# Scheduling priority for the RWKV chains, solves and chunk operands of a hybrid mLSTM and RWKV-7 layer

## Chip, cores and metric

The kernel runs on one core of a Trainium2 chip. The metric is the device time of one execution in microseconds (us), here the median of the runs. Engines: PE = TensorE (matmuls), DVE = VectorE, ACT = ScalarE, POOL = GpSimd, SP = SyncE, whose queue issues the DMAs.

## What is computed

One layer of a diffusion backbone with 512 latent tokens (x), 256 context tokens (ctx) and a width of 2048. Cut to what matters:

```python
sh1, sc1, gt1, sh2, sc2, gt2 = adaln(c, w_mod, b_mod)         # six vectors of 2048; w_mod is 2048 x 12288
hc = modulate(rms_norm(ctx, g_norm1), csh1, csc1)
_, ctx_state = hybrid_mixers(hc, p, zero_state)
hx = modulate(rms_norm(x, g_norm1), sh1, sc1)
yx, _ = hybrid_mixers(hx, p, ctx_state)
x = x + gt1 * (yx @ w_out)
x = x + gt2 * conv_ffn(modulate(rms_norm(x, g_norm2), sh2, sc2))
return rms_norm(x, g_final)

def hybrid_mixers(h, p, state):
    proj = h @ p["w_in"]                  # all inputs of both head groups
    ...                                   # 4 mLSTM heads, 16 RWKV-7 heads, both in two directions

def rwkv7_step(s, r, w, k, v, kk, a):     # for each token and head, state 64 x 64
    s = s * w[None, :] - (s @ kk)[:, None] * (kk * a)[None, :] + v[:, None] * k[None, :]
    return s, s @ r
```

## The kernel before

All data are fp32. A dense product splits the weights and the tokens into a high and a low part and takes three matmuls (`proj` L362 ff. with the lines L370 to L372, `proj_tm` with L403 to L405 and others). The weights come through `wload` (L337): a DMA into `wraw`, then the split into `whi` on ACT (L299) and `wlo` on DVE (L300).

RWKV runs over pairs of heads (8 pairs) and chunks of 64 tokens in these stages:

- `pair_shared` and `prep` (L680) make a pair's operands for all chunks: decays from a scan (`r_cum`), exponentials, and the products of chunk operands (`r_Gp`, L747). They store them in DRAM as `Sx_d` (latent tokens) or `Sc_d` (context).
- `tsolve` (L777) inverts the triangular matrices of four units at once: eight loads into `t_X`, thirty steps of two DVE operations each (L798 multiplies, L799 adds), eight stores (L801). Then, for each pair, it loads `t_Y` (L808), transposes on DVE (L810), and joins the halves by small matmuls on PE (L816, L821) with the copy L823, and stores (L824).
- `chain` (L903) runs the recurrence. `chain_v` loads the values, `chain_load` (L826) loads `r_GK` for two chunks, and `chain_step` (L841) computes one chunk in three dependent groups of 64x64 matmuls (L856, L859), with copies to `r_Rs` and `r_U` on ACT (L872, L880) between them. The state `r_M` (L892) and the outputs `r_yt` (L899, L901) are updated on DVE.
- `finalize_pair` (L944) normalises a pair's outputs.

The six vectors of `adaln` come from two kinds of code. The first come early from PE. The others are `ada_late` (L219) chunks: eight loads `am` (L228, one buffer) from `w_mod`, each followed by two DVE products into `adacc` (L230, L232), and at the end a sum over partitions on PE (L238) with L239 on DVE. The sum of a chunk is issued when two later chunks are waiting.

Which job comes when is set by `ctx_job` and `x_job` and the main loop at the end of the mixers. Within a job the program is not the order on the engines: the scheduler of the Tile framework lists all operations by simulated time, and among ready ones takes those with the higher priority, by default the earlier in the program. `tc.high_priority(n)` puts what is inside it n places ahead of its place in the program. In the kernel before, `wload` uses it with 3000 (`AHEAD`, `AHEAD_X`). Each engine then works through its own list in order.

After the last dense projection of the inputs come the last chain, the four mLSTM heads (L540; head 0 runs beside the last chain: L605, L609, L621, L641), the output projection (L1262 ff.) and the convolution FFN.

Of the kernel before, what the change touches and what calls it, by code (L numbers as in the profile page):

```python
# [15 lines left out]
P = 128  # L16
# [70 lines left out]
FIN_O = 1  # L87
EARLY_AT = (1, 2, 4, 4)
PRELOAD = True
TCOPT = dict(schedule_with_timeline_sim=True)  # L90


# [4 lines left out]
def body(tc, A, dbg=None):  # L97
# [5 lines left out]
    def nm(s):  # L103
        cnt[0] += 1
        return f"{s}_{cnt[0]}"
# [25 lines left out]
    def DT(tag, shape, bufs=1):  # L131
        return dr.tile(list(shape), F32, tag=tag, name=nm(tag), bufs=bufs)
# [31 lines left out]
    def V(name, j=0, n=1):  # L164
        o = VO[name] + j
        return vecs[:, o:o + n]
# [74 lines left out]
    def ln_exp():  # L241

        if PRELOAD:
            tc.keep_in_program_order(act.preload_act_table_set("natural_log_exp_and_others"))
# [414 lines left out]
    def pair_shared(p, seg):  # L659
        n = NX if seg == "x" else NC_  # L660
        s = K()
        s.kr = rp("r_kr", [P, NX])
        s.kk = rp("r_kk", [P, NX])
        sp.dma_start(s.kr[:, :n], kr_d[seg][p])
        act.activation(s.kk[:, :n], s.kr[:, :n], AF.Copy, scale=V("rkk", p))
        sq = rp("r_t1", [P, NX])
        act.activation(sq[:, :n], s.kk[:, :n], AF.Square)
        pn = PS("pre", [P, 512])
        pe.matmul(pn[:, :n], bones, sq[:, :n], start=True, stop=True)
        act.activation(sq[:, :n], pn[:, :n], AF.Ln, bias=BK12)  # L670
        act.activation(sq[:, :n], sq[:, :n], AF.Exp, scale=-0.5)
        dve.tensor_tensor(s.kk[:, :n], s.kk[:, :n], sq[:, :n], ALU.mult)
        if seg == "x":
            s.r = rp("r_r", [P, NX])
            sp.dma_start(s.r, r_d[p])
        s.up = rp("r_up", [P, 2, 2, P])
        sp.dma_start(s.up, A["rup"][p])
        return s
# [147 lines left out]
    def chain_load(u, tt):  # L826

        cu = u.c0 + 2 * tt
        o = rk("r_GK", [P, 2, 512], 6)[:, :, 0:3 * u.kc + 128]
        sp.dma_start(o, u.S_d[:, cu:cu + 2, :])  # L830
        return o

    def chain_v(p, seg, nch):

        t = rk("r_V", [P, 8, 64], 3)[:, 0:nch]
        for h, hs in enumerate(LOHI):
            o = (p % 2) * 128 + 64 * h
            sp.dma_start(t[hs], v_d[seg][p // 2, :, :, o:o + 64].rearrange("a (b t) v -> t (a b) v", t=64))
        return t

    def chain_step(us, ops, cs, V, y, first, last):  # L841

        x = us[0].seg == "x"
        kc = us[0].kc
        bank = [PS("R", [P, 8, 64]) for _ in range(2)]
        pos = (0, 1) if cs[0] < cs[1] else (1, 0)
        opened = {}

        def mm(h, half, o, w, rhs):

            hs = LOHI[h]
            out = bank[h][LOHI[half], o, :]
            at = opened.get((h, half))
            f = dict(stop=True, skip_group_check=True)
            if at is None:
                opened[(h, half)] = pe.matmul(out, w[hs], rhs[hs], start=True, **f)  # L856
                return
            with tc.issue_after(at.ins):
                pe.matmul(out, w[hs], rhs[hs], start=False, **f)  # L859

        w = [o[:, c % 2] for o, c in zip(ops, cs)]
        kinds = range(2) if x else range(1)
        for src in range(2):
            for k, u in enumerate(us):
                for j in kinds:
                    for h in range(2):
                        o = 2 * kc * src + 64 * j
                        mm(h, h if j == 0 else 1 - h, pos[k], w[k][:, o:o + 64], u.M if src == 0 else V[:, cs[k], :])
        Rs = rk("r_Rs", [P, 2, 64], 3)
        U = rk("r_U", [P, 2, 64], 3)  # L870
        for h, hs in enumerate(LOHI):
            act.copy(Rs[hs], bank[h][hs, 0:2, :])  # L872
        for k, u in enumerate(us):
            for h in range(2):
                mm(h, 1 - h, 2 + pos[k], w[k][:, kc:kc + 64], Rs[:, pos[k], :])
            for h in range(2):
                if not last:
                    mm(h, h, 2 + pos[k], w[k][:, 3 * kc + 64:3 * kc + 128], V[:, cs[k], :])
        for h, hs in enumerate(LOHI):
            act.copy(U[hs], bank[h][LOHI[1 - h], 2:4, :])  # L880
        for k, u in enumerate(us):
            for h in range(2):
                if not last:
                    mm(h, h, 2 + pos[k], w[k][:, 3 * kc:3 * kc + 64], U[:, pos[k], :])
            for h in range(2):
                if x:
                    mm(h, 1 - h, pos[k], w[k][:, kc + 64:kc + 128], U[:, pos[k], :])
        if not last:
            for k, u in enumerate(us):
                g = u.g0 + cs[k]  # L890
                for h, hs in enumerate(LOHI):
                    dve.scalar_tensor_tensor(u.M[hs], u.M[hs], u.gC[hs, g:g + 1], bank[h][hs, 2 + pos[k], :], ALU.mult, ALU.add)  # L892
        if x:
            lo, hi = min(cs), max(cs)
            for h in range(2):
                hs = LOHI[1 - h]
                out = y[hs, lo:hi + 1:hi - lo, :]
                if first:
                    dve.tensor_copy(out, bank[h][hs, 0:2, :])  # L899
                else:  # L900
                    dve.tensor_tensor(out, bank[h][hs, 0:2, :], out, ALU.add)  # L901

    def chain(pairs, mid):  # L903

        x = pairs[0][0].seg == "x"
        nch = pairs[0][0].nch
        Vs, ys = [], []
        for us in pairs:
            Vs.append(chain_v(us[0].p, us[0].seg, nch))
            ys.append(rk("r_yt", [P, 8, 64], 2) if x else None)  # L910
            for u in us:
                if not x:
                    Mst[(u.p, u.d)] = rk("r_M", [P, 64], 16)
                    pool.memset(Mst[(u.p, u.d)], 0.0)
                u.M = Mst[(u.p, u.d)]
        n = nch // 2
        for i in range(n):
            if x and i == 1:
                mid()
            ops = [[chain_load(u, i if u.d == 0 else n - 1 - i) for u in us] for us in pairs]  # L920
            for c in range(2 * i, 2 * i + 2):
                for us, o, V, y in zip(pairs, ops, Vs, ys):
                    chain_step(us, o, (c, nch - 1 - c), V, y, c < nch // 2, x and c == nch - 1)
        if x:
            for us, y in zip(pairs, ys):
                y_d = us[0].y_d = DT("yr_d", [4, P, 128], 8)
                for h in range(2):
                    sp.dma_start(y_d[:, :, 64 * h:64 * h + 64].rearrange("a (b t) v -> t (a b) v", t=64), y[LOHI[1 - h]])
            mid()

    def bonus(p, uf, ub, s):
        kd = uf.kd
        dve.tensor_tensor(kd, kd, ub.kd, ALU.add)
        dve.tensor_tensor(kd, kd, s.r, ALU.mult)
        rk2 = rk("r_rk2", [P, 2], 2)
        pool.tensor_scalar(rk2, bones2, V("rrk", p), None, ALU.mult)
        pb = PS("pre", [P, 4, 2])
        for tt in range(4):
            pe.matmul(pb[:, tt, :], kd[:, 128 * tt:128 * tt + 128], rk2, start=True, stop=True)
        bo = rk("r_bo", [P, 8], 6)  # L940
        act.copy(bo, pb.rearrange("p a b -> p (a b)"))
        return bo
# [140 lines left out]
    for q, (k0, k1) in enumerate(KPARTS):  # L1083
        ks = slice(k0, k1)
        n = (k1 - k0) * P
# [53 lines left out]
    def do_solve(n=1):  # L1139
        if len(solve_q) >= n:  # L1140
            jobs = [solve_q.pop(0) for _ in range(n)]
            tsolve([us for job in jobs for _, us, _ in job])
            chain_q.extend(jobs)

    def ctx_job(p):
        do_chain()
        job = []
        for pp in range(p, p + 2):
            s = pair_shared(pp, "c")
            job.append((pp, prep(pp, s, "c", DT("Sc_d", [P, 8, 320], 8)), None))  # L1150
        do_solve()
        solve_q.append(job)

    def x_job(p):
        if p < 2:
            do_chain()
        elif p % 2 == 0:
            do_solve(2)
        else:
            do_chain(2)  # L1160
        s = pair_shared(p, "x")
        S_d = DT("Sx_d", [P, 16, 512], 8)
        us = prep(p, s, "x", S_d, 0) + prep(p, s, "x", S_d, 1)
        job = [(p, us, bonus(p, us[0], us[1], s))]
        if p == 0:
            do_solve()
        solve_q.append(job)
# [186 lines left out]
    for g in range(NG):  # L1354
# [7 lines left out]
        for cs in (slice(0, NX),) if g < NG - 1 else (slice(0, NX // 2), slice(NX // 2, NX)):  # L1362
            n = cs.stop - cs.start
# [137 lines left out]
```

## Time and profile before

| | |
|---|---|
| median of 3 runs | 3376.26 us (3374.53 to 3378.07) |
| profiled execution | 3379.97 us |
| its span | 3378.2 us |
| mean granted clock of TensorE | 0.945 |
| busy: PE, DVE, ACT, POOL | 92%, 64%, 35%, 2% |
| read from and written to HBM | 457.49 MB, 87.47 MB |

The profile is of one execution; its times are from the start of the span. A busy share is the time that instructions of an engine ran, as a share of a stretch. The clock is the part of full speed that the chip granted TensorE. A row of the timeline has the start, the duration, the engine, the line, the operation with what it writes and reads, and in brackets the idle time of the engine before it with what ended that. A row of waits has the engine, its line, the engine and line it waited for, the total in us, the number of waits and the longest. SPq is the queue of SP. In the table of windows each engine has its busy time and, in brackets, its instructions; the last three columns are PE's clock, the busy share of the DMA engines and GB/s.

### The profile page before, as it was taken

Reading aid. Unit: us, or ns where it says so; the run is one execution under the profiler, and the core shown is the slowest. Engines: PE = TensorE matmul, PEld = TensorE weight load, DVE = VectorE, ACT = ScalarE, POOL = GpSimd, SP = SyncE. Lnnn points to the kernel's source line nnn. Section 1 sums busy time; section 2 is a strip of 40 time slices with the busy share of each in tenths; the row PEclk is TensorE's granted clock in tenths of the full one; section 3 lists DMA queues with packets and bytes.
Section 4 is the critical chain, followed back from the end, with each engine's and each line's share of the span. In section 5 each row is a group of like instructions: output and inputs, shape, how many; then the busy total and the mean of one; then the engine's idle time right before and its main releaser. Section 6 shows DMA issues by size and latency. Waiting matters only on the chain.

```text
span 3378.2 us, 54574 instructions
## 1 busy us (share of the span) xinstructions
PE 3108.0 (92%) x21030; PEld 2509.7 (74%) x21030; DVE 2165.9 (64%) x4178; ACT 1192.4 (35%) x2414; POOL 59.6 (2%) x113
## 2 busy tenths in 40 slices
PE   8998899999989898657599899999999999999998
PEld 5687777777768687545477688888888888888887
DVE  2587776688688778645644788455555555555657
ACT  4355554344444344222223432222222222322323
POOL 0000100010000000000000000000000000000000
PEclk9999998899989898767799999999999999999999
DMA  8877555557767687565844255222223222222232
GB/s 284 305 243 220 155 159 163 166 174 234 208 208 239 215 247 240 181 197 178 257 153 157 77 199 194 94 94 98 95 95 99 94 96 98 94 98 96 94 100 100
DMA packets 394387, 548.53 MB, mean 162 GB/s; under 512 B 151664, under 2 KB 272776, under 8 KB 393872
## 3 DMA queue, kind: packets, MB, share of 16 engines
q1 hardware_dynamic: 384480, 531.67, 49.3%
q10 hardware_dynamic: 9648, 13.37, 1.1%
q8 instruction: 166, 2.72, 0.3%
q14 instruction: 93, 0.76, 0.1%
HBM read 457.49 MB, written 87.47 MB: 161 GB/s over the span
## 4 chain that ended last, share of the span: by engine, by line
PE 53%; DMA 9%; DVE 6%; ACT 1%; issue 1%; SPq 1%; DVEq 0%; ACTq 0%
PE acc L371 10%; PE acc L372 10%; PE acc L370 10%; PE acc L1376 5%; PE acc L1378 5%; PE acc L1377 5%; DMA am<-in_wmod 3%; PE acc L1262 1%; PE pre L621 1%; PE acc L1263 1%; PE acc L1264 1%; DVE adacc L232 1%; DMA Sx_d<-r_sg 1%; PE R L859 1%; DMA x_d<-ev 1%
## 5 line engine op out<-in xcount | busy, mean ns | idle before, releaser
L299 ACT CAST whi<-wraw 128x512 fp32r<-128x512 f32 (+1 forms) x948 | 569.6, 604 | 1307.7 <-PE acc L371 678.6
L300 DVE TENSOR_TENSOR wlo<-wraw,whi 128x512 fp32r<-128x512 f32 (+1 forms) x948 | 628.4, 666 | 429.0 <-ACT whi L299 423.1
L370 PE MATMUL acc<-H,whi 128*128 128x512 f32 x1920 | 761.2, 396 | 6.1 <-ACT ev L520 4.0
L372 PE MATMUL acc<-H,wlo 128*128 128x512 f32 x1920 | 762.3, 397 | 1.2 <-DVE wlo L300 1.2
L371 PE MATMUL acc<-H,whi 128*128 128x512 f32 x1920 | 760.4, 396 | 0.0
L370 PEld LDWEIGHTS acc<-H,whi 128*128 128x128 f32 x1920 | 363.8, 189 | 87.5 <-ACT ev L520 4.3
L372 PEld LDWEIGHTS acc<-H,wlo 128*128 128x128 f32 x1920 | 364.2, 190 | 82.0 <-issue 4.9
L371 PEld LDWEIGHTS acc<-H,whi 128*128 128x128 f32 x1920 | 364.4, 190 | 78.8 <-issue 2.9
L1380 DVE SCALAR_TENSOR_TENSOR x<-acc,mod,x 128x512 f32<-128x512 f32 (+1 forms) x192 | 135.6, 706 | 221.7 <-PE acc L1378 221.6
L1324 DVE SCALAR_TENSOR_TENSOR f_cv<-upad,fvec,f_cv 128x512 f32<-128x512 f32 x352 | 263.8, 749 | 7.2
L1376 PE MATMUL acc<-fh,whi 128*128 128x512 f32 x640 | 253.2, 396 | 0.0
L1377 PE MATMUL acc<-fl,whi 128*128 128x512 f32 x640 | 253.1, 396 | 0.0
L1378 PE MATMUL acc<-fh,wlo 128*128 128x512 f32 x640 | 253.1, 396 | 0.0
L232 DVE SCALAR_TENSOR_TENSOR adacc<-am,csil,adacc 128x512 f32<-128x512 f32 x240 | 179.4, 748 | 83.7 <-DMA am<-in_wmod 81.6
L403 PE MATMUL acc<-whi,H 128*128 128x256 f32 x512 | 159.8, 313 | 2.2 <-ACT r_E L720 1.5
L405 PE MATMUL acc<-wlo,H 128*128 128x256 f32 x512 | 158.6, 311 | 1.6 <-DVE wlo L300 1.6
L404 PE MATMUL acc<-whi,H 128*128 128x256 f32 x512 | 156.0, 305 | 0.0
L1378 PEld LDWEIGHTS acc<-fh,wlo 128*128 128x128 f32 x640 | 120.2, 188 | 29.1
L1377 PEld LDWEIGHTS acc<-fl,whi 128*128 128x128 f32 x640 | 120.2, 188 | 29.0
L1376 PEld LDWEIGHTS acc<-fh,whi 128*128 128x128 f32 x640 | 120.2, 188 | 29.0
L1262 PE MATMUL acc<-H,whi 128*128 128x512 f32 x256 | 104.6, 414 | 32.4 <-DVE ev L1271 18.6
L750 DVE TENSOR_TENSOR r_Gp<-pre,c_gmask 64x512 f32<-64x512 f32 (+1 forms) x192 | 115.1, 599 | 18.1 <-DMA Sx_d<-r_Gp 11.6
(346 smaller groups left out, 4751.6 us busy)
## 6 DMA issues: line engine op xcount, KB each, us to landing
am<-in_wmod SPq DMA_DIRECT2D x128, 512.0 KB
wraw<-in_wup SPq DMA_DIRECT2D x88, 512.0 KB
wraw<-in_wgate SPq DMA_DIRECT2D x88, 512.0 KB
wraw<-in_wdn SPq DMA_DIRECT2D x88, 512.0 KB
wraw<-in_wcm SPq DMA_DIRECT2D x72, 512.0 KB
r_GK<-Sx_d SPq DMA_DIRECT2D x64, 512.0 KB
wraw<-in_wtm SPq DMA_DIRECT2D x56, 512.0 KB
Sx_d<-r_Gp SPq DMA_DIRECT2D x32, 512.0 KB
```

Of the source, the lines that this page charges most:

```text
L232: dve.scalar_tensor_tensor(acc, wm[:, k % 2], csil[:, k:k + 1], acc, ALU.mult, ALU.add)
L299: act.copy(hi, t)
L300: dve.tensor_tensor(lo, t, hi.bitcast(F32), ALU.subtract)
L370: pe.matmul(pt[:, :n], hi(k8), H.h(k), start=k == 0, stop=False)
L371: pe.matmul(pt[:, :n], hi(k8), H.l(k), start=False, stop=False)
L372: pe.matmul(pt[:, :n], lo(k8), H.h(k), start=False, stop=k == KT - 1)
L403: pe.matmul(o, H.h(k)[:, xs], hi(k4), start=first, stop=False, skip_group_check=True)
L405: pe.matmul(o, H.h(k)[:, xs], lo(k4), start=False, stop=k == KT - 1, skip_group_check=True)
L1324: dve.scalar_tensor_tensor(cv, u[:, a:a + GH, b:b + GW], fvec[:, f, tap:tap + 1], cv, ALU.mult, ALU.add)
L1376: pe.matmul(pt, hi(m)[:, k, :], th[:, cs], start=k == 0, stop=False)
L1377: pe.matmul(pt, hi(m)[:, k, :], tl[:, cs], start=False, stop=False)
L1378: pe.matmul(pt, lo(m)[:, k, :], th[:, cs], start=False, stop=k == GF - 1)
```

## The change

Two constants are added, and `tc.high_priority` is put around `chain_v`, `chain_load` and `chain_step`, around `tsolve`, and around `pair_shared`, `prep` and `bonus`. Dense products, `finalize_pair`, the mLSTM heads and `ada_late` keep their priority.

```diff
+AHEAD_C = 3000
+AHEAD_P = 1500
...
         for us in pairs:
-            Vs.append(chain_v(us[0].p, us[0].seg, nch))
+            with tc.high_priority(AHEAD_C):
+                Vs.append(chain_v(us[0].p, us[0].seg, nch))
...
-            ops = [[chain_load(u, i if u.d == 0 else n - 1 - i) for u in us] for us in pairs]
-            for c in range(2 * i, 2 * i + 2):
-                for us, o, V, y in zip(pairs, ops, Vs, ys):
-                    chain_step(us, o, (c, nch - 1 - c), V, y, c < nch // 2, x and c == nch - 1)
+            with tc.high_priority(AHEAD_C):
+                ops = [[chain_load(u, i if u.d == 0 else n - 1 - i) for u in us] for us in pairs]
+                for c in range(2 * i, 2 * i + 2):
+                    for us, o, V, y in zip(pairs, ops, Vs, ys):
+                        chain_step(us, o, (c, nch - 1 - c), V, y, c < nch // 2, x and c == nch - 1)
...
             jobs = [solve_q.pop(0) for _ in range(n)]
-            tsolve([us for job in jobs for _, us, _ in job])
+            with tc.high_priority(AHEAD_C):
+                tsolve([us for job in jobs for _, us, _ in job])
...
         for pp in range(p, p + 2):
-            s = pair_shared(pp, "c")
-            job.append((pp, prep(pp, s, "c", DT("Sc_d", [P, 8, 320], 8)), None))
+            with tc.high_priority(AHEAD_P):
+                s = pair_shared(pp, "c")
+                job.append((pp, prep(pp, s, "c", DT("Sc_d", [P, 8, 320], 8)), None))
...
-        s = pair_shared(p, "x")
-        S_d = DT("Sx_d", [P, 16, 512], 8)
-        us = prep(p, s, "x", S_d, 0) + prep(p, s, "x", S_d, 1)
-        job = [(p, us, bonus(p, us[0], us[1], s))]
+        with tc.high_priority(AHEAD_P):
+            s = pair_shared(p, "x")
+            S_d = DT("Sx_d", [P, 16, 512], 8)
+            us = prep(p, s, "x", S_d, 0) + prep(p, s, "x", S_d, 1)
+            job = [(p, us, bonus(p, us[0], us[1], s))]
```

The added lines move the lines behind them by 2 (before `chain`) up to 7; below, L856 of before is L858 of the change, and so on. The order of the instructions is shown at three places.

The first is PE at the chain of the first two latent pairs, at the start of one of its steps (`R` is the step's PSUM bank, `r_M` the state, `acc` a dense product). Before:

```order
L370 MATMUL acc_10839<-H_2686,whi_10880 128x512
L371 MATMUL acc_10839<-H_2687,whi_10880 128x512
L856 MATMUL R_7513<-r_M_7469,r_GK_7477 64x64
L856 MATMUL R_7514<-r_M_7469,r_GK_7477 64x64
L856 MATMUL R_7545<-r_M_7462,r_GK_7473 64x64
L859 MATMUL R_7513<-r_M_7471,r_GK_7479 64x64
```

And with the change:

```order
L405 MATMUL acc_10593<-whi_10601,H_2680 128x256
L406 MATMUL acc_10593<-whi_10601,H_2681 128x256
L858 MATMUL R_7513<-r_M_7469,r_GK_7477 64x64
L858 MATMUL R_7514<-r_M_7469,r_GK_7477 64x64
L858 MATMUL R_7545<-r_M_7462,r_GK_7473 64x64
L858 MATMUL R_7546<-r_M_7462,r_GK_7473 64x64
```

The same step has moved ahead, from the middle of one dense product (acc_10839) into an earlier one (acc_10593).

The second is SP's queue at the stores of the last solve (`Sx_d` from `t_X`) and the `am` loads of two `ada_late` chunks (am_13718 is the last load of one, am_15321 the first of the next). Before:

```order
L228 DMA am_13718<-in_wmod 128x1024
L967 DMA r_y_14749<-g_d_123 128x512
L228 DMA am_15321<-in_wmod 128x1024
L228 DMA am_15325<-in_wmod 128x1024
L228 DMA am_15329<-in_wmod 128x1024
L801 DMA Sx_d_12429<-t_X_13722 16x32x32 x4
L801 DMA Sx_d_13495<-t_X_13722 16x32x32 x4
L808 DMA t_Y_13802<-Sx_d_12429 128x16x64
```

And with the change:

```order
L230 DMA am_13718<-in_wmod 128x1024
L803 DMA Sx_d_12429<-t_X_13722 16x32x32 x4
L803 DMA Sx_d_13495<-t_X_13722 16x32x32 x4
L810 DMA t_Y_13802<-Sx_d_12429 128x16x64
L230 DMA am_15321<-in_wmod 128x1024
L230 DMA am_15325<-in_wmod 128x1024
L826 DMA Sx_d_12429<-t_Y_13802 2048x1x64
L230 DMA am_15329<-in_wmod 128x1024
```

The eight stores and the first load of `t_Y` stood behind three loads of the next chunk and now stand ahead of them.

The third is DVE at the same place (L799 is a solve step's second operation, L230 and L232 the products of `am`, L239 the end of an `ada_late` chunk). Before, the end of the thirty steps:

```order
L232 SCALAR_TENSOR_TENSOR adacc_15320<-am_15325,csil_110,adacc_15320 128x512
L798 TENSOR_TENSOR t_T_13731<-t_X_13722 128x84
L609 SCALAR_TENSOR_TENSOR r_BK_15940<-pre_16008,r_BK_15940 128x384
L609 SCALAR_TENSOR_TENSOR r_kk_15933<-pre_16008,r_kk_15933 128x256
L799 TENSOR_TENSOR t_X_13722<-t_X_13722,t_T_13731 128x3x28
L798 TENSOR_TENSOR t_T_13731<-t_X_13722 128x58
L799 TENSOR_TENSOR t_X_13722<-t_X_13722,t_T_13731 128x2x29
L798 TENSOR_TENSOR t_T_13731<-t_X_13722 128x30
L799 TENSOR_TENSOR t_X_13722<-t_X_13722,t_T_13731 128x30
```

And with the change:

```order
L800 TENSOR_TENSOR t_T_13731<-t_X_13722 128x58
L801 TENSOR_TENSOR t_X_13722<-t_X_13722,t_T_13731 128x2x29
L800 TENSOR_TENSOR t_T_13731<-t_X_13722 128x30
L801 TENSOR_TENSOR t_X_13722<-t_X_13722,t_T_13731 128x30
L234 SCALAR_TENSOR_TENSOR adacc_13689<-am_13718,csil_110,adacc_13689 128x512 x2
L241 TENSOR_TENSOR mod_112<-pre_15893,c_vecs_88 128x4
```

The last step stood behind products of the second load of the next chunk, and now stands ahead of the products of the last load of the chunk before.

## Rows read from the trace of the kernel before

**Rows 1.** The page, part 1: busy time, share of the span, instructions.

```profile
PE 3108.0 (92%) x21030; PEld 2509.7 (74%) x21030; DVE 2165.9 (64%) x4178; ACT 1192.4 (35%) x2414; POOL 59.6 (2%) x113
```

**Rows 2.** The table of windows.

```profile
core 0: us, PE busy (x) PEld busy (x) DVE busy (x) ACT busy (x) POOL busy (x), PEclk, DMA share, GB/s
280.00:726.00 446.00, 409.16 (x3343) 335.32 (x3344) 327.71 (x768) 214.23 (x467) 35.96 (x38) 0.94 0.55 164
726.00:946.00 220.00, 203.27 (x2089) 167.29 (x2088) 166.14 (x342) 90.23 (x200) 7.90 (x12) 0.96 0.72 219
946.00:1280.00 334.00, 306.82 (x3581) 246.33 (x3581) 266.05 (x596) 147.64 (x329) 5.65 (x15) 0.93 0.75 234
1280.00:1402.00 122.00, 108.89 (x1242) 90.63 (x1242) 90.28 (x220) 49.32 (x125) 2.15 (x5) 0.86 0.67 212
1402.00:1590.00 188.00, 113.14 (x1435) 80.50 (x1434) 105.87 (x271) 40.11 (x133) 0.21 (x2) 0.66 0.58 183
...
1943.00:3378.00 1435.00, 1418.67 (x6395) 1171.45 (x6394) 854.27 (x1311) 407.24 (x677) 0.00 (x0) 1.00 0.32 108
```

**Rows 3.** The table of waits of PE, 280 to 1402 us.

```profile
PE pre L759 <- DVE r_cum L756: 10.6, 4, 6.3
PE R L859 <- ACT r_U L880: 10.4, 9, 1.7
PE pre L747 <- DVE r_Gp L750: 9.3, 13, 1.7
...
PE R L859 <- ACT r_Rs L872: 3.8, 4, 1.5
```

**Rows 4.** The chain of waits by line: 1402 to 1470 us, then 1470 to 1590.

```profile
by line: DMA am<-in_wmod 43.6%; DVE adacc L232 15.9%; SPq L801 7.0%; DMA t_Y<-Sx_d 6.5%; PE R L821 4.6%; DMA r_y<-v_x 4.2%; DVE t_X L799 3.1%; PE R L816 2.9%; issue 2.3%; DVE t_Y L823 2.0%; DVE t_T L798 2.0%; DVE r_BK L609 1.6%; DVE t_X L81
...
by line: DMA am<-in_wmod 29.4%; PE pre L621 16.3%; DVE adacc L232 11.7%; DMA t_X<-rows_d 4.3%; DMA r_BK<-rows_d 4.2%; SPq L587 3.9%; DMA hm_d<-r_r 3.7%; DMA r_r<-so_d 3.3%; issue 3.1%; DVE r_M L892 3.1%; DMA ev<-hm_d 2.6%; DVE r_yt L901 1.7
```

**Rows 5.** The instructions of L228, 1402 to 1590 us.

```profile
L228 SPq DMA_DIRECT2D am<-in_wmod x28: 327/333/1422, 1405.6 to 1585.3; - x28
```

**Rows 6.** The timeline of PE at the last solve.

```profile
1424.95 1.84 PE L238 MATMUL pre<-c_ones,adacc 128*128 128x1 f32 x8 [22.87 <-DVE adacc L232]
1426.65 3.76 PE L605 MATMUL pre<-r_kr,r_KR 128*128 128x512 f32 x4
...
1447.87 1.92 PE L816 MATMUL R<-t_X,t_Y 32*32 32x32 f32 x64 [9.65 <-DVE t_X L810]
...
1466.63 0.49 PE L856 MATMUL R<-r_M,r_GK 64*64 64x64 f32 x8
```

**Rows 7.** The instructions of L901, 1580 to 1600 us.

```profile
L901 DVE TENSOR_TENSOR r_yt<-R,r_yt x6: 282/288/294, 1580.9 to 1589.7; 64x128 f32<-64x128 f32 x6
```

**Rows 8.** The timeline of PE inside a chain step, 797 to 803 us.

```profile
797.97 0.45 PE L859 MATMUL R<-r_V,r_GK 64*64 64x64 f32 x8
...
799.54 0.39 PE L370 MATMUL acc<-H,whi 128*128 128x512 f32 x1
...
802.30 0.39 PE L370 MATMUL acc<-H,whi 128*128 128x512 f32 x1
802.62 0.27 PE L856 MATMUL R<-r_Rs,r_GK 64*64 64x64 f32 x1
```

**Rows 9.** The timeline of DVE, three places between 1369 and 1437 us.

```profile
1369.06 0.48 DVE L230 TENSOR_SCALAR adacc<-am,csil 128x512 f32<-128x512 f32 x1
...
1423.10 0.75 DVE L232 SCALAR_TENSOR_TENSOR adacc<-am,csil,adacc 128x512 f32<-128x512 f32 x1 [2.25 <-DMA am<-in_wmod]
...
1436.95 0.19 DVE L799 TENSOR_TENSOR t_X<-t_X,t_T 128x30 f32<-128x30 f32 x1
```

**Rows 10.** The timeline of SP's queue, 1424 to 1443 us.

```profile
1424.83 10.60 SPq L228 DMA_DIRECT2D am<-in_wmod  x3
1437.17 5.04 SPq L801 DMA_DIRECT2D Sx_d<-t_X  x8
1442.37 0.58 SPq L808 DMA_DIRECT2D t_Y<-Sx_d  x1
```

## The prediction

> **What bounds the kernel now.** I began with the page: TensorE (PE) is busy 92% of the 3378.2 us span [rows 1]. The kernel is bound by dense matmuls, and a new order of the same work can only take away idle time of PE or time at a low clock. Where those lie is shown by the table of windows [rows 2]. I cut it where before and after have finished the same set of instructions, or at an event. From 1943 us on PE is busy 1418.67 of 1435 us at a clock of 1.00: nothing can be won there. From 280 to 1402 us, where the dense projections run beside the RWKV chains, four windows are busy 409.16 of 446, 203.27 of 220, 306.82 of 334 and 108.89 of 122 us. Idle are 36.8 + 16.7 + 27.2 + 13.1 = **94 us**, over 1122 us. From 1402 to 1590 us the dense products are used up: PE is busy 113.14 of 188 us at a clock of 0.66. I call this stretch the tail.
>
> What PE waits for before 1402 us stands in the table of waits [rows 3]. The three longest sums are r_cum (10.6 us in 4 waits, one of 6.3), r_U of the chains (10.4 us in 9) and r_Gp (9.3 us in 13). They are many small waits, no single one; all are for operands of RWKV work, which the change touches.
>
> The tail reads differently. In the chain of waits, 43.6% of 1402 to 1470 us is the load of `am`, 15.9% the products on VectorE (DVE) that read it; of 1470 to 1590 us 29.4% and 11.7% [rows 4]. `am` has one buffer, so a load starts when both products of the one before are done. The rows of L228 show 28 loads from 1405.6 to 1585.3 us, hence 179.7 / 27 = 6.66 us for each [rows 5]. DVE works in the order of its queue. So whatever stands behind such a product also waits for the load. That the last chain is paced by it shows in its length: 16 steps from the first L856 at 1466.63 [rows 6] to the last L901 at 1589.7 us [rows 7], 7.7 us a step.
>
> **The change, part by part.** No operation is added or removed on PE, DVE, SP and POOL; ACT loses two table loads, which I cost at nothing since ACT is busy for 35% [rows 1]. What changes is the order, from about 270 to 1590 us. The sets of finished instructions agree again at the window edges 726, 946 and 1280 us. Behind 1590 us the order is the same. So gains and losses are made inside windows.
>
> *Before the tail.* The largest move on PE is 249 rows, at the chain of the first latent pairs, near 797 us. In the old order one step's first products end at 797.97 + 0.45, the next ones start at 802.62 us, and dense products fill the time between [rows 8]: nothing is idle there. Moving that step forward shifts equal work past equal work and gives nothing by itself. It pays where PE waits now, and costs where a chain product comes to the head before its operand is there. Bounds come from rows. Gain: the 94 us of idle time can't all go, since the three longest sums (10.6 + 10.4 + 9.3) are only 30 us. Loss: in the new order shorter runs of dense products stand between the stages of a chain step at more places; if the waits for r_U (10.4) and r_Rs (3.8 us in 4) double [rows 3], that is **+14 us**. I take **0**: the engine that makes these operands, DVE, is busy 73 to 80% of these windows [rows 2] with the same work, and what is computed sooner for the chain delays the split of weights that the dense products need. Ends kept: -30 and +14.
>
> The Trainium skill, page "PSUM — Partial Sum Buffer", section "Engine vs sequencer instructions", says that matmuls start and complete in program order. This speaks against putting chain products early: one that isn't ready would hold all the dense ones behind it, and by that rule alone the term would be the loss. The trace agrees that such holding happens: L238 waits 22.87 us at 1424.95 us with ready L605 behind it [rows 6]. It doesn't show that the new places are too early.
>
> *The solve in the tail.* Before, the last of the thirty solve steps (L799) runs at 1436.95 us, behind two loads of the next chunk [rows 9]. Now all thirty stand ahead of the eighth product pair of the chunk before, whose load lands at 1423.10 us in the old run. The start of this am loop is later, though: the first use of its loads (L230) ran at 1369.06 us [rows 9] and has moved about 20 DVE rows back, behind L239, and PE's L238 that feeds L239 has moved 34 rows back, behind the last dense products, which follow each other every (802.30 - 799.54) / 12 = 0.23 us [rows 8]: 34 x 0.23 = 8 us at most, nothing at least; I take 5. So the last L799 comes at about 1423 + 5 = 1428 us. From its end to the first L816 it was 1447.87 - 1437.14 = 10.7 us, for eight stores (5.04 us of SP's queue), the load of t_Y and its transposition [rows 6, 9, 10]. Hence L816 at 1438.7 us; the L238 and four L605 ahead of it on PE take 1.84 + 3.76 us after the last product of am (1.5 us after L799), and are through by about 1435. That is **9 us earlier**, and the chain's first products come as much earlier, near 1458 us.
>
> *What is moved past on SP.* The first two am loads of the next chunk now stand behind the eight stores and the load of t_Y. They were issued from 1424.83 us; now after 1428 + 5.04 + 0.58 = 1433.6 us, plus the wait for L799's signal: **10 us later** [rows 10].
>
> *Which of the two sets the end of the tail.* The chain's steps stand among the am products on DVE, and in the new order two to three loads further ahead: the last rows of r_yt, of the chain and the first stores of mLSTM head 0 come after load 6 of that chunk where it was load 8. Two to three times 6.66 us are 13.3 to 20 us. With the loop 10 us late, the end moves by 10 - 13.3 = -3.3 to 10 - 20 = -10 us. The other end is +10, if the head's own operands, and not the chain, wait for the loads. I take **-4**, near the smaller gain, because the chain of waits gives am in 1470 to 1590 us more than any other [rows 4].
>
> **Sum.** 0 - 4 = -4 us against the profiled execution's own 3379.97 us: 3376. The median of the runs shown is 3.7 us below that execution, so I forecast 3376.26 - 4 = **3372 us**. A measurement here can tell about 0.2%, 6.8 us, from no change; the forecast lies inside it.
>
> **The rivals.**
> *1. The waits before the tail do get covered (faster).* A third of the 94 us, 31 us, goes (about the bound above), and the tail gives its -8. For it: every wait of [rows 3] is for work that gets priority, and dense products are left to fill. Against it: they are small and DVE is nearly full. 3376 - 39 = **3337 us**. It could be more by the clock: these four windows run at 0.94, 0.96, 0.93 and 0.86 [rows 2]; at full clock their busy time would be shorter by 0.06 x 409 + 0.04 x 203 + 0.07 x 307 + 0.14 x 109 = 69 us, a third of which is 23: 3314. The same Trainium skill, page "Perfetto Trace Analysis", section "Matmul Optimizations", says that the matmul engine scales power with use and wants batches back to back; the trace agrees as far as 0.66 goes with the emptiest window and 1.00 with the fullest.
>
> *2. The am loop keeps the tail, and PE stalls at early chain products (slower).* Place: SP's am loads behind the solve's stores, +10 to the end if the first use of the loads is what head 0 and the chain wait for; and +14 before, with the in-order stalls. From the point at which the am products come later by more than the solve comes earlier, 9 us, it decides. For it: am is the largest share of the tail's chain of waits. Against it: the chain now stands ahead of two loads more. 3376 + 24 = **3400 us** for both, 3386 for the loop alone.
>
> *3. The change does nothing that counts.* Weight loads already run at the priority given now, PE's rows move by 249 at most of 16700, and the order is equal again at every window's edge: **3376 us**.
>
> **How the numbers follow.** Forecast 0.50 (of it 0.18 faster by over 0.2%, 0.24 within, 0.08 slower, as its terms spread from -10 to +10); rival 1 0.22; rival 2 0.19; rival 3 0.09. Faster 0.18 + 0.22 = 0.40; same 0.24 + 0.09 = 0.33; slower 0.08 + 0.19 = 0.27. The range holds the forecast with its ends, rival 1 with some of its clock gain, and rival 2: 3325 to 3400 us. The forecast's own range is 3362 to 3386.
>
> **What would show it.** Right: in the windows before 1402 us PE's idle sum stays at 94 us within 15; L816 of the last solve starts 8 us earlier against the end of the dense products; the first am load of that chunk follows the eight stores; the last L901 comes some 4 us earlier, and everything after 1590 us is shifted as a whole. Wrong: idle before 1402 below 70 us or a clock that rises there (rival 1); waits at L859 and L856 that double, or a last L901 later than 1600 us (rival 2); a last L816 at the old place (rival 3).

## The result and the profile after

The changed kernel takes 3398.93 us (median of 3 runs, 3394.86 to 3405.27), before 3376.26 us: a ratio of 1.0069, with an interval of 1.0043 to 1.0096. It is **slower by 0.7%**; a second set of runs (below) gave 1.0087 (1.0068 to 1.0106). The profiled execution took 3394.86 us with a span of 3393.1 us, 14.9 us more than the one before.

The first part of the page after, beside [rows 1]: PE works for almost the same time (3105.5 us for 3108.0) in a longer span.

```profile
PE 3105.5 (92%) x21030; PEld 2512.8 (74%) x21030; DVE 2169.2 (64%) x4178; ACT 1191.2 (35%) x2412; POOL 50.0 (1%) x113
```

Where the time went shows when both traces are cut at points where PE has finished the same instructions in both orders. First the table of windows of the kernel before, cut there (the columns are those of [rows 2]; the edges of [rows 2] themselves lie some 11 us behind these points, which I had wrong in the prediction):

```profile
275.10:715.70 440.60, 403.21 (x3318) 330.91 (x3317) 323.69 (x761) 213.66 (x467) 36.84 (x40) 0.94 0.54 162
715.70:858.60 142.90, 135.62 (x1105) 110.50 (x1104) 117.52 (x249) 55.42 (x122) 8.26 (x9) 0.96 0.74 224
...
907.80:1268.90 361.10, 328.62 (x3934) 266.71 (x3933) 286.25 (x646) 154.34 (x354) 6.21 (x17) 0.92 0.74 230
1268.90:1383.90 115.00, 101.73 (x1318) 83.14 (x1317) 84.15 (x199) 50.81 (x129) 2.15 (x5) 0.85 0.71 231
1383.90:1449.80 65.90, 31.38 (x169) 21.16 (x167) 46.18 (x109) 10.26 (x18) 0.00 (x0) 0.66 0.52 155
1449.80:1591.60 141.80, 100.56 (x1355) 74.84 (x1356) 73.47 (x194) 37.45 (x129) 0.21 (x2) 0.71 0.60 194
```

The same stretches of work in the kernel after:

```profile
276.20:709.40 433.20, 400.33 (x3321) 331.32 (x3320) 325.30 (x777) 209.80 (x462) 23.52 (x38) 0.94 0.55 163
709.40:858.40 149.00, 135.85 (x1103) 110.91 (x1102) 118.08 (x238) 56.48 (x124) 3.73 (x9) 0.97 0.71 218
...
906.20:1278.50 372.30, 333.98 (x3930) 271.62 (x3929) 279.09 (x621) 151.85 (x349) 15.51 (x17) 0.93 0.71 218
1278.50:1409.70 131.20, 101.13 (x1318) 83.11 (x1317) 92.56 (x226) 54.27 (x133) 0.94 (x5) 0.86 0.70 213
1409.70:1461.70 52.00, 27.98 (x199) 20.39 (x199) 40.55 (x96) 11.78 (x20) 0.00 (x0) 0.74 0.60 176
1461.70:1604.40 142.70, 98.53 (x1332) 73.44 (x1329) 76.71 (x198) 37.06 (x128) 0.21 (x2) 0.75 0.61 199
```

Row by row the change gives -7.4, +6.1, (the row left out: -1.4), +11.2, **+16.2**, **-13.9** and +0.9 us. In the row with +16.2 PE's work is the same (101.73 and 101.13 us) and its idle time goes from 13.3 to 30.1 us. (At 1461.7 us the change is 34 of L823's small products further than the kernel before at 1449.8; with the cut at 1460.7 us, where the sets are equal, the last two are -14.9 and +1.9.) So the change loses 25 us before the dense products end and wins 13 back behind them; a further 2 us go behind 1591 us and 1 us ahead of 275.

The waits of PE show where that idle time lies. Before, two lines of the table for 1269 to 1384 us:

```profile
PE R L859 <- ACT r_U L880: 3.8, 3, 1.4
...
PE R L856 <- DVE r_yt L899: 1.1, 3, 0.5
```

After, the longest sums of the table for 1278 to 1410 us (L858 is L856 of before, L240 is L238, L749 is L747):

```profile
PE R L858 <- DVE r_yt L901: 8.2, 9, 4.0
PE pre L240 <- ACT r_sg L765: 6.5, 1, 6.5
PE R L858 <- DVE r_yt L903: 3.2, 5, 1.7
PE pre L749 <- DVE r_BK L738: 2.9, 1, 2.9
```

The chain's products (L858) and the operands' (L749), which got priority, now stand at the head of PE's order before their data or their PSUM bank is there. L240 is the end of an `ada_late` chunk and got no priority; its 6.5 us are a wait for the operands' copy `r_sg`.

In the tail, the rows that answer to [rows 6, 7]:

```profile
1450.21 1.84 PE L240 MATMUL pre<-c_ones,adacc 128*128 128x1 f32 x8 [23.20 <-DVE adacc L234]
...
1458.10 1.20 PE L818 MATMUL R<-t_X,t_Y 32*32 32x32 f32 x64
...
1477.30 0.49 PE L858 MATMUL R<-r_M,r_GK 64*64 64x64 f32 x8
...
L903 DVE TENSOR_TENSOR r_yt<-R,r_yt x5: 282/283/295, 1591.5 to 1599.5; 64x128 f32<-64x128 f32 x5
```

And those that answer to [rows 10], SP's queue:

```profile
1444.78 0.33 SPq L230 DMA_DIRECT2D am<-in_wmod  x1
1447.12 4.94 SPq L803 DMA_DIRECT2D Sx_d<-t_X  x8
1452.22 0.61 SPq L810 DMA_DIRECT2D t_Y<-Sx_d  x1
1452.87 7.74 SPq L230 DMA_DIRECT2D am<-in_wmod  x2
```

The solve's stores stand ahead of the next chunk's loads, as the order says. But the last solve's first L818 comes at 1458.10 us, 10 us later than 1447.87 [rows 6], and not 9 us earlier.

### The profile page after: what moved, and what is told of

Its sections match the earlier page's. It is cut to its first block, busy times and chain, and to the rows that moved or that the text cites. A ratio compares the mean times of both kernels' runs of the same rounds, so it can differ in the third digit from the quotient of the medians.

```text
span 3393.1 us, 54558 instructions
## 1 busy us (share of the span) xinstructions
PE 3105.5 (92%) x21030; PEld 2512.8 (74%) x21030; DVE 2169.2 (64%) x4178; ACT 1191.2 (35%) x2412; POOL 50.0 (1%) x113
## 4 chain that ended last, share of the span: by engine, by line
PE 47%; DMA 7%; DVE 4%; ACT 1%; issue 1%; SPq 1%; DVEq 0%; ACTq 0%
PE acc L372 9%; PE acc L373 9%; PE acc L374 9%; PE acc L1383 5%; PE acc L1384 5%; PE acc L1385 5%; DMA am<-in_wmod 2%; PE acc L1269 1%; PE acc L1270 1%; PE acc L1271 1%; PE pre L623 1%; DMA x_d<-ev 1%; DVE adacc L234 1%; DMA hm_d<-r_r 0%; DMA wraw<-in_wdn 0%
## 5 line engine op out<-in xcount | busy, mean ns | idle before, releaser
L372 PE MATMUL acc<-H,whi 128*128 128x512 f32 x1920 | 760.1, 396 | 5.7 <-ACT ev L522 4.7
L372 PEld LDWEIGHTS acc<-H,whi 128*128 128x128 f32 x1920 | 364.4, 190 | 85.4 <-ACT ev L522 5.0
L405 PE MATMUL acc<-whi,H 128*128 128x256 f32 x512 | 154.2, 302 | 2.1 <-DVE srsr L271 1.0
L406 PE MATMUL acc<-whi,H 128*128 128x256 f32 x512 | 154.6, 302 | 0.0
L752 DVE TENSOR_TENSOR r_Gp<-pre,c_gmask 64x512 f32<-64x512 f32 (+1 forms) x192 | 115.1, 599 | 55.8 <-DMA Sx_d<-r_Gp 20.4
```

The source lines that it names most:

```text
L372: pe.matmul(pt[:, :n], hi(k8), H.h(k), start=k == 0, stop=False)
L406: pe.matmul(o, H.l(k)[:, xs], hi(k4), start=False, stop=False, skip_group_check=True)
```

## The experiments

One number turned out to follow the losses: when the **operands of the last latent pair** (pair 7) are ready, read as the start of the last L759 (L761 of the change) in the instructions of that line. Before and with the change, for 1250 to 1440 us:

```profile
L759 PE MATMUL pre<-c_ident,r_cum x16: 272/273/473, 1313.5 to 1364.4; 128*128 128x128 f32 x16
...
L761 PE MATMUL pre<-c_ident,r_cum x24: 270/273/473, 1256.3 to 1390.3; 128*128 128x128 f32 x24
```

The last one starts 25.9 us later. After `prep` of pair 7 come the last solve and the last chain. I formed four theories:

- A: operands that come early hold DVE's queue, and the chain waits.
- B: chain products placed early hold PE's queue (rival 2 of the prediction).
- C: the scheduler's order is so tightly wound that any large change of it costs or wins at random.
- D: the kernel is bound, up to the tail, by the latency chain from one pair's operands to the next pair's (mostly one set of buffers, some 85 us a pair; in the trace of before 65 to 92 us, with gaps of 7 to 42 us between pairs), then the last solve and the tail. What gets in its way costs, and when the dense products end doesn't matter. This one I formed after the first four runs.

Ratios below are to the old kernel run beside it. The edits are to the changed kernel, where not said otherwise; `nullcontext()` in place of `tc.high_priority(...)` gives a part its default priority back.

**The change again.** No edit.

> The whole change once more, as the yardstick of this set. All theories: 15 to 25 us slower than before (it was 22.7 us by the medians, 14.9 by the profiled executions), with PE idle for 110 to 125 us between the points where both orders have done the same instructions at about 275 and 1384 us of before (94 us before).

Measured: 3399.86 us, 1.0087 (1.0068 to 1.0106), 27.1 us by the medians, a little above the 15 to 25 expected; PE is idle for 114 us between the two points, as expected. The loss stands.

**Chains alone**, with solve and operands back at the default:

```diff
-            with tc.high_priority(AHEAD_C):
+            with nullcontext():
                 tsolve([us for job in jobs for _, us, _ in job])
...
-            with tc.high_priority(AHEAD_P):
+            with nullcontext():
                 s = pair_shared(pp, "c")
...
-        with tc.high_priority(AHEAD_P):
+        with nullcontext():
             s = pair_shared(p, "x")
```

> Priority only for chain_v, chain_load and chain_step; solve and operands as before. Theory A (the operands of prep come early, wait for the one buffer of r_Gp and for their DMAs, and hold DVE's queue, behind which the chain's r_yt and r_M wait): within 6 us of before. Theory B (chain matmuls placed early hold PE's queue): 12 to 25 us slower, with waits of L858 for r_yt and of L861 for r_U at least doubled. Theory C (any large change of the list order costs, whatever is moved): 5 to 15 us slower.

Measured: 3391.63 us, 1.0062 (1.0038 to 1.0086). At 19 us slower this fits B, not A, and is a little more than C had. Two things didn't fit B: of the two waits that should have doubled, between 700 and 1440 us, L858's for r_yt did (25.3 us, before 5.7) and L861's for r_U didn't (8.9, before 7.9); and PE finished its dense products 40 us *sooner* than before (last start 1362.1 us, before 1401.7), while the kernel was slower.

**Solves alone:** the same for the operands, and for `chain_v`, `chain_load` and `chain_step` in place of `tsolve`.

```diff
-            with tc.high_priority(AHEAD_C):
+            with nullcontext():
                 Vs.append(chain_v(us[0].p, us[0].seg, nch))
...
-            with tc.high_priority(AHEAD_C):
+            with nullcontext():
                 ops = [[chain_load(u, i if u.d == 0 else n - 1 - i) for u in us] for us in pairs]
```

> Priority only for tsolve. Theories A and B: 5 to 14 us faster, since the last solve ends earlier against the last dense product and the loss before it isn't made (the change itself won 13.9 us between the equal points at 1383.9 and 1449.8 us of before). Theory C: 5 to 15 us slower.

Measured: 3409.18 us, 1.0116 (1.0098 to 1.0133), 36 us slower. A and B are both wrong here, and it is more than C gave.

**Operands alone:** both edits above, for chains and for `tsolve`, and the operands keep 1500.

```diff
-            with tc.high_priority(AHEAD_C):
+            with nullcontext():
                 tsolve([us for job in jobs for _, us, _ in job])
```

> Priority only for pair_shared, prep and bonus. Theory A: 15 to 30 us slower, DVE's waits at r_Gp (L752) for the store of r_Gp above 15 us between 700 and 1400 us. Theory B: within 6 us of before. Theory C: 5 to 15 us slower.

Measured: 3364.06 us, 0.9974 (0.9958 to 0.9991): slightly faster, by 8.7 us of the medians. **Theory A falls**: the part that I held for the culprit is the one that helps. B (within 6 us) and C (slower) miss it too. Operands of pair 7 were ready at 1347.9 us (before 1364.4; chains alone 1381.2; solves alone 1386.5). That led to D, and the next set was made against it.

**Operands alone, at 3000:**

```diff
-AHEAD_P = 1500
+AHEAD_P = 3000
```

> Operands alone, with a priority of 3000 in place of 1500. Theory D (the latency chain from the operands of one latent pair to those of the next, about 85 us each, ends with the last solve and the tail; whoever delays it loses, whoever shortens it wins, and when the dense products end doesn't matter): the operands of pair 7 are done (last L759 of before) before 1355 us and the kernel is 5 to 35 us faster than before. Theory C (any other order costs or wins at random): no relation to the first run with operands alone; as likely slower as faster.

Measured: 3358.92 us, 0.9964 (0.9945 to 0.9982); operands at 1346.1 us. As D said.

**The whole change, with the operands ahead of chains and solves:**

```diff
-AHEAD_P = 1500
+AHEAD_P = 6000
```

> The whole change with the operands at 6000 and chains and solves at 3000, so that the operands go first. Theory D: most of the loss goes; operands of pair 7 done by 1365 us, within 8 us of before or faster. Theory B (early chain products and solves cost by themselves): still 12 to 30 us slower.

Measured: 3365.92 us, 0.9982 (0.9968 to 0.9996); operands at 1359.0 us. One number turns the loss of 0.9% into a gain of 0.2%, with all chain products and solves still at 3000. Against B, for D.

**Chains and solves without the operands:** `nullcontext()` around the operands only.

```diff
-        with tc.high_priority(AHEAD_P):
+        with nullcontext():
             s = pair_shared(p, "x")
```

> Chains and solves alone. Theory D: the operands are delayed most, pair 7 done after 1385 us, 18 to 40 us slower, the worst or next to the worst of all. Theory C: anywhere from -10 to +40.

Measured: 3429.34 us, 1.0171 (1.0156 to 1.0186), 58 us slower, more than D had; operands at 1418.0 us, the latest of all. With chains and solves at 3000 throughout, three ranks of the operands now stand in a row: at the default 1418.0 us and 1.0171, at 1500 1385.7 and 1.0087, at 6000 1359.0 and 0.9982. This is the clearest sign that the loss comes with the rank of the operands against chains and solves.

**Operands of the latent pairs only:** as operands alone, and without the context's.

```diff
-            with tc.high_priority(AHEAD_P):
+            with nullcontext():
                 s = pair_shared(pp, "c")
```

> Priority 1500 for the operands of the latent pairs only, not for those of the context. Theory D: the first latent pair begins 15 to 20 us later than with both, since the context jobs aren't brought forward, but its chain is as fast: within 8 us of before, at best 10 us faster. If the context's share doesn't matter: 5 to 15 us faster, as with both.

Measured: 3358.88 us, 0.9962 (0.9947 to 0.9977). The context's share doesn't matter; what I had D say of it was wrong: the lead of some 20 us that the first latent pair has with both is lost later: with either, some 60 to 70 us pass between pair 4's last operand product and pair 5's first, where it was 12 us before. Pair 5's own dense products aren't what is awaited there. With the latent operands alone they were stored by 746 us, loaded at 993 and 995 us, and ACT's first step on them (L667) ran at 998.8 us, but the next product on PE (L671) at 1067.5; with the context's too, L667 ran at 978.6 and L671 at 1070.0 us, right behind a product of `finalize_pair` (L975) for which PE had been idle for 14.3 us. In the kernel before, the two steps lie 30 us apart (1025.4 and 1055.7 us). So pair 5 stands behind other work in PE's order there; why the scheduler puts it there is open.

**Latent operands, and the last solve:** a flag that only the last call of `do_solve` sets.

```diff
-            with tc.high_priority(AHEAD_C):
+            with tc.high_priority(AHEAD_C) if last else nullcontext():
                 tsolve([us for job in jobs for _, us, _ in job])
...
-    do_solve(2)
+    do_solve(2, True)
     for h in range(MH):
```

> Priority for the latent operands (1500) as in the run before with them alone, and priority 3000 for the last solve only, behind which no operands follow. Theory D: the solve costs only where operands of a later pair stand behind it, so the last one is free or wins; against latent operands alone 0 to 12 us faster, against before 12 to 25 us faster, the last L799 before 1395 us. If a solve with priority costs by itself: 8 to 30 us slower than operands alone.

Measured: 3369.13 us, 0.9999 (0.9989 to 1.0009). A miss: the last solve's first L816 came at 1413.5 us, 4 us later than with the latent operands alone (1409.6), and the rest of the gain is gone behind it. Against these it is 12 us slower by the ratios, as the other theory had (a solve with priority costs by itself); the last solve alone, below, speaks against that one.

**The same and the last chain**, by the same flag in `do_chain`:

```diff
-            do_chain(2)
+            do_chain(2, True)
```

> The same with priority for the last chain too. Theory D: against the latent operands alone 0 to 15 us faster. If chain products placed early cost by themselves (theory B): 8 to 20 us slower than with the last solve alone.

Measured: 3367.74 us, 0.9986 (0.9975 to 0.9997). D misses again, some 8 us slower by the ratios than the latent operands alone, and so does B: it isn't slower than with the last solve alone.

**The last solve and the last chain alone:** as above, with default priority for all operands.

```diff
-        with tc.high_priority(AHEAD_P):
+        with nullcontext():
             s = pair_shared(p, "x")
```

> The last solve and the last chain alone; the order before the last solve as in the old kernel. Theory D: 0 to 14 us faster than before (the change won 13.9 us between the equal points at 1383.9 and 1449.8 us). Theory B: 5 to 15 us slower than before.

Measured: **3348.65 us, 0.9937 (0.9915 to 0.9959)**, 21 us faster than before by the medians, the fastest of all and more than D had.

**The old kernel again**, for a second profile:

> The old kernel itself, for a second profiled execution. All theories: no difference by the rounds. The last solve's first L816 within 8 us of the 1447.9 us of the first profile.

Measured: 3368.60 us, 1.0005 (0.9989 to 1.0022). Its profiled execution has a span of 3365.4 us, where the first had 3378.2, and the last solve's first L816 at 1439.4 us (first: 1447.9), a little more than the 8 us expected. So a split by stretch from one profile each is good to some 10 us; the +16 and -14 above stand clear of that, the small ones don't. The second profiles of both kernels, cut at the same points, repeat the main split: the change is some 27 us longer up to the point at 1383.9 us of the first profile and 14 us shorter from there to the one at 1449.8.

**The last solve alone**, and **the last chain alone** (one flag each):

```diff
-    do_solve(2)
+    do_solve(2, True)
```

> Priority for the last solve alone. Theory D: no operands stand behind it, so it wins what the solve ends earlier: 5 to 20 us faster. If a solve with priority costs by itself: 5 to 20 us slower.

Measured: 3350.56 us, 0.9968 (0.9953 to 0.9982), 15 us faster by the medians, as D said.

```diff
-            do_chain(2)
+            do_chain(2, True)
```

> Priority for the last chain alone. Theory D: 0 to 10 us faster, most of the gain of both comes from the solve. Theory B: 5 to 15 us slower.

Measured: 3357.01 us, 0.9970 (0.9954 to 0.9986), 8 us by the medians. By the ratios each gives about half of what both give. The intervals of the two overlap almost wholly, so that most comes from the solve isn't borne out.

**The dense products first**, and no priority for RWKV: the opposite of the change, made to tell a bound of dense products from one of latency.

```diff
         if p + 1 < NPAIR:
-            x_pair(p + 1)
+            with tc.high_priority(AHEAD_P):
+                x_pair(p + 1)
```

> No priority for RWKV; the dense products of the next latent pair (values, k and r) get 1500 instead. Theory D: the dense products end earlier than the 1402 us of before, but the operands of pair 7 are done later than 1364.7, and the kernel is 5 to 40 us slower. If the kernel is bound by the dense products (PE busy 92%): faster or the same.

Measured: 3422.64 us, 1.0193 (1.0162 to 1.0224), 57 us slower by the medians, the way D said and more than its 40. The instructions of three lines in this run, up to 1480 us (L405 and L372 are dense products, L403 and L370 of before; L761 makes the operands):

```profile
L405 PE MATMUL acc<-whi,H x36: 274/283/415, 1200.0 to 1244.3; 128*128 128x256 f32 x36
...
L372 PE MATMUL acc<-H,whi x32: 387/389/793, 1247.8 to 1286.1; 128*128 128x512 f32 x32
...
L761 PE MATMUL pre<-c_ident,r_cum x32: 272/421/477, 1259.8 to 1407.7; 128*128 128x128 f32 x32
```

The same of the fastest run, last solve and last chain alone:

```profile
L372 PE MATMUL acc<-H,whi x96: 387/390/504, 1215.2 to 1408.9; 128*128 128x512 f32 x96
...
L761 PE MATMUL pre<-c_ident,r_cum x16: 273/374/474, 1295.9 to 1341.0; 128*128 128x128 f32 x16
```

With dense products first, these end at 1286 us, 115 us sooner than before, and the kernel loses 57 us; in the fastest run they end at 1409 us. Behind 1287 us the first of the two has nothing to fill PE with, as its windows show (PE is busy 73.05 of 121 us at a clock of 0.55 until the operands are ready):

```profile
700.00:1287.00 587.00, 546.70 (x5540) 448.76 (x5538) 458.37 (x973) 249.74 (x551) 16.74 (x33) 0.96 0.69 215
1287.00:1408.00 121.00, 73.05 (x1101) 57.77 (x1101) 83.09 (x179) 37.91 (x97) 0.60 (x4) 0.55 0.66 205
```

**All runs together**, each from its profiled execution, in us from the span's start:

| priority for | operands of pair 7 (last L759) | last solve, first L816 | last dense product of the inputs | span | ratio |
|---|---|---|---|---|---|
| none (before) | 1364.4 | 1447.9 | 1401.7 | 3378.2 | |
| none, again | 1356.9 | 1439.4 | 1394.3 | 3365.4 | 1.0005 |
| all (the change) | 1390.3 | 1458.1 | 1425.4 | 3393.1 | 1.0069 |
| all, again | 1385.7 | 1455.6 | 1423.2 | 3395.6 | 1.0087 |
| chains | 1381.2 | 1448.8 | 1362.1 | 3382.6 | 1.0062 |
| solves | 1386.5 | 1479.9 | 1449.4 | 3412.5 | 1.0116 |
| chains and solves | 1418.0 | 1487.4 | 1403.3 | 3426.5 | 1.0171 |
| dense products | 1407.7 | 1480.3 | 1286.5 | 3421.1 | 1.0193 |
| all, operands first | 1359.0 | 1433.1 | 1389.0 | 3371.4 | 0.9982 |
| operands, 1500 | 1347.9 | 1416.7 | 1375.0 | 3353.4 | 0.9974 |
| operands, 3000 | 1346.1 | 1427.2 | 1409.8 | 3363.5 | 0.9964 |
| latent operands | 1337.3 | 1409.6 | 1415.2 | 3359.4 | 0.9962 |
| latent operands, last solve | 1345.0 | 1413.5 | 1424.1 | 3373.4 | 0.9999 |
| latent operands, last both | 1340.3 | 1409.0 | 1419.6 | 3366.0 | 0.9986 |
| last solve | 1343.6 | 1415.5 | 1383.9 | 3342.1 | 0.9968 |
| last chain | 1340.1 | 1404.7 | 1413.7 | 3357.3 | 0.9970 |
| last solve and chain | 1341.0 | 1403.3 | 1409.3 | 3347.2 | 0.9937 |

Over the 17 profiles the span follows the second column (correlation 0.94) and the third (0.94), and not the last dense product (-0.17). The differences of span and L816 lie between 1926 and 1960 us, while L816 itself moves by 84 us. But the second column parts the slow runs from the fast ones and doesn't rank the fast ones: among the eight with operands before 1350 us, which lie within 11 us there, the spans still differ by 31 us, and the correlation is 0.03 (with the last dense product 0.70). So D accounts for the losses; which of the gains is larger it doesn't tell, and behind L816 up to 34 us are won or lost by something else.

**How the operands are held up** shows in the trace of the change, beside a chain and a solve of the context. The timeline of PE, 443 to 450 us (L749 makes products of the operands, L858 is the chain's):

```profile
442.95 1.10 PE L749 MATMUL pre<-r_KR,r_BK 64*128 64x64 f32 x14
...
448.61 0.65 PE L858 MATMUL R<-r_Rs,r_GK 64*64 64x64 f32 x3 [4.16 <-ACT r_Rs L874]
...
449.52 0.68 PE L749 MATMUL pre<-r_KR,r_BK 64*128 64x64 f32 x2
```

The timeline of ACT there (L667 begins the next pair's operands, L874 copies the chain's `r_Rs`):

```profile
447.76 0.51 ACT L667 ACTIVATE r_kk<-r_kr,c_vecs 128x256 f32<-128x256 f32 x1 [4.63 <-DMA r_kr<-kr_c]
448.30 0.55 ACT L874 COPY r_Rs<-R 64x128 f32<-64x128 f32 x2
```

And that of DVE (L800 and L801 are steps of a solve, L752 takes the operands' products out of PSUM):

```profile
450.21 0.86 DVE L752 TENSOR_TENSOR r_Gp<-pre,c_gmask 64x256 f32<-64x256 f32 x2
451.10 0.31 DVE L801 TENSOR_TENSOR t_X<-t_X,t_T 64x150 f32<-64x150 f32 x1
...
459.31 1.75 DVE L752 TENSOR_TENSOR r_Gp<-pre,c_gmask 64x256 f32<-64x256 f32 x4
```

The sixteen products of half a pair are cut in two: fourteen run at once; the last two stand behind a chain product that was moved up among them. That one waits 4.16 us for its copy, and the copy stands in ACT's queue behind an L667 that waits 4.63 us for a load; L667 was itself moved up. So L749 goes on at 449.52, L752 starts at 450.21, shares DVE with a solve, and the pair's last four start at 459.31 us. From the pair's first L749 to there it is 16.4 us. In the old order PE has no such wait at the same pair, whose second half reads so (L747 is L749 of the change, L750 is L752):

```profile
438.36 0.89 PE L747 MATMUL pre<-r_KR,r_BK 64*128 64x64 f32 x12
...
440.41 0.44 PE L747 MATMUL pre<-r_KR,r_BK 64*128 64x64 f32 x4
...
440.88 1.75 DVE L750 TENSOR_TENSOR r_Gp<-pre,c_gmask 64x256 f32<-64x256 f32 x4 [1.30 <-PE pre L747]
```

From its first L747, at 428.9 us, to these last four it is 12.0 us. So this place costs 4.4 us, about the wait. It is one place; that it is the pattern behind the whole delay is argued from the runs, not counted through.

## Why the prediction was wrong

- **What bounds the kernel** is the step that failed: "The kernel is bound by dense matmuls". PE's share of 92% and the small sums of its waits [rows 1 to 3] were read as a bound. The run with dense products first shows that their end isn't what sets the time: they ended 115 us sooner and the kernel was 57 us slower. The dense products fill PE while a chain of latencies runs, operands of pair 0 to pair 7, last solve, tail. I followed that chain in the tail only, where PE was visibly empty.
- **Term "before the tail"**: taken as 0, with ends of -30 and +14. By the equal points it is about +25 us (1383.9 us of before is 1409.7 us after; some 27 in the second profiles), and nearly all of it is idle time of PE. I had bounded it by the waits of PE that were there, doubled. What early chain products hold up and what counts aren't the dense products but the operands, which are made later (by 26 us) because the list gives solves and chains 3000 and operands 1500: at 6000 for the operands the loss is gone. The reason for 0, that DVE has the same work, overlooked that the *order* of the work is what the operands wait for.
- **The solve in the tail**: mechanism right, its place wrong. Between the equal points around it the change wins some 14 us, where I had 9. But I started it from the old times (1428 us for the last L799); it ran at 1446.9 us, since the operands were 26 us late.
- **SP's queue and the end of the tail**: order as read, and the loads of the next chunk do follow the stores. From the first L816 of the last solve to the last L901 the tail is as long as it was (141.8 and 141.4 us), where I had it some 5 us longer (9 us gained at the solve, 4 at the end); the last L901 came 9.8 us later and not 4 earlier.
- **Forecast and rivals**: forecast 3372 us, measured 3399, which the range (to 3400 us) still held, though the sign was wrong. Rival 2 gave 3400 us, and that it came so close is luck: it had +14 before the tail and +10 in it, where +25 and -13 were measured. Its mechanism is only in part the one found: waits at L858 for r_yt did appear (8.2 us in 9 waits between 1278 and 1410 us), but with the operands put first and chains and solves still at 3000, the loss is gone. The rule of the Trainium skill, page "PSUM — Partial Sum Buffer", section "Engine vs sequencer instructions", that matmuls go in program order, was right to speak against the change; the trace agrees with 4.16 us at 448.61 us, and what stood behind was an operand's product. The sentence before it in that section of the Trainium skill has ScalarE's queue as strict FIFO, and the 4.63 us of L667 with a ready copy behind it agree.
- **Rival 1** (waits covered, clock up): idle PE time before the dense end rose, from 94 to 117 us between the equal points. The clock stayed within 0.01 of what it was in each of these windows.

**Still open:** why the gains of the latent operands and of the last solve and chain don't add (0.9962 and 0.9937 apart, 0.9986 together); and why with the last solve, the last chain or both the operands of pair 7 were ready 13 to 24 us sooner, though their own priority is the old one. So these gains can't be put down to the solve and the chain alone. A shift of the whole list is part of any such edit; theory C isn't out for differences of some 10 us.

## What to carry to other kernels

A busy share of 92% doesn't prove a bound: give the work that fills the engine priority over the rest once, and see whether the end moves. Before raising the priority of several stages, find the one on the chain that sets the end (here the operands) and rank the others below it. The last solve and the last chain, raised by themselves, won 0.6% here, and all solves and chains together lost 1.7%; but with the latent operands raised as well most of the gain was lost, so what wins alone has to be measured again together. Where engines work in order, hurrying a stage can put its waits for DMAs ahead of ready work, as the 4.63 us of L667 show.

## What was not expected of the hardware

One kernel's executions spread more than the three first runs showed: the old one took 3351 to 3377 us over 25 runs in one set, 0.8%, at mean granted clocks of 0.943 to 0.951. And with the dense products first the granted clock fell from 0.96 to 0.55, close to the lower of its two levels (1.2 of 2.4 GHz), for 121 us in which PE was busy for 73.05. Whether that clock cost anything isn't shown: PE stood idle for 48 us of the stretch, but the operands' products (L761) took 421 ns in the median, where they took 374 in the fastest run.
